# The end of FFN 1 in a hybrid encoder layer: T4 by adding transfers, and the next weights' splits placed around the norms

## The chip, the cores and the metric

The kernel runs on one core of one Trainium2 chip. The metric is the device time of one execution in microseconds; lower is better. It is 1113.76 us before the change (median of 3 runs, 1113.51 to 1113.84).

## The reference

One layer of a streaming encoder on 512 tokens of width 1024, all in float32:

```python
f = swiglu(rms_norm(h, ffn1_pre_g), ffn1_w1, ffn1_w3, ffn1_w2)     # (silu(x@w1) * (x@w3)) @ w2, d_ff 2816
h = h + 0.5 * rms_norm(f, ffn1_post_g)
u = rms_norm(h, mix_pre_g)
q, k, v, xr, xg = split(u @ w_in)
...                                                                # RG-LRU branch, windowed attention, gates, w_o
h = h + 0.5 * rms_norm(swiglu(rms_norm(h, ffn2_pre_g), ...), ffn2_post_g)
```

The change lies in the seam `f @ w2`, the two norms behind it, and the first products of `u @ w_in` (its columns xr).

## The kernel before, in words

**Precision.** Every float32 operand is split into a high and a low part of the matrix format: ScalarE (ACT) copies the high part, VectorE (DVE) subtracts it for the low part. A product is then three matmuls, high x high, high x low, low x high. A 128 x 1024 piece of weights so costs one ACT pass and one DVE pass before TensorE (PE) can use it. `split_dma` makes the low part without VectorE: ACT writes the high part and the negated raw piece, and a DMA from GpSimd's queue (POOL) adds the raw piece from HBM onto it. The set `BY_DMA` names the pieces that are split so.

**Storage.** All big tiles come from one pool of 42 slots of 4 KB a partition. A slot that is asked for while it is still in use makes the asking engine or queue wait for its last user.

**The down projection w2 of FFN 1** is done by seven products of a Strassen-Winograd scheme on halves of the tokens and of the output columns, in the order m1, m5, m2, m6, m3, m7, m4. Each product is cut into G = 5 units of 12 matmuls. `step(u)` prepares units up to u + 4 (`prep(u + LEAD)`, LEAD = 5), runs what `hooks[u]` holds, and then issues the matmuls of unit u; so m1 is steps 0 to 4, m5 5 to 9, m2 10 to 14, m6 15 to 19, m3 20 to 24, m7 25 to 29, m4 30 to 34. Preparing a unit is: split the weights' side (L659 ACT `whi`, L667 DVE `wlo`), split the tokens' side (L213 ACT, L214 DVE), and form the sums and differences that later products need (`sums`). Of the weights' differences, T1 and T2 are made by adding transfers here (`T_load`: L596 ACT negates, L597 POOL's DMA adds), T3 (`b11`) and T4 (`b21`, formed as the units of m6 are prepared) by a DVE pass each (L589). T2 overwrites b22, so m3 loads b22 anew (L673). Two tiles of w2 (2 and 3, `tail`) are multiplied in the plain way (`classical`, L242 to L244).

**The norms.** A tile of 128 tokens is complete when m1 to m6 and the tail (tiles 0 and 1) or m4 and the tail (tiles 2 and 3) are in. `norm(t)` is then one chain over VectorE and ScalarE: add the parts (L294), square and sum (L296), reciprocal root (L259 to L264), new h (L308), square and sum again (L320), root, scaled u (L331 DVE, L332 ACT). PE transposes u (L341), ACT and DVE copy it out as high and low (L351, L353), ACT copies it once more for later (L361). With queues in order, whatever stands in ACT's or DVE's queue ahead of a norm's instruction delays the norm. The order is written out by hand:

- steps 0 to 24; tail on tiles 0 and 1; unit 29 prepared; norm(0);
- steps 25 to 29 (m7); its sum is taken out by DVE (L700), after which m4 may use the banks;
- tail, one column half, on tiles 2 and 3; unit 34 prepared; norm(1);
- m4 on tile 2, transposes of tile 0, tail, norm(2); m4 on tile 3, transposes of tile 1, tail;
- `start`: products with xr0 on the first 256 tokens, transposes of tile 2, norm(3), xr1, one eighth of xr2, transposes of tile 3, the rest of xr2, then the columns 256 to 512 of xr0 and xr1 and so on (L224 to L226).

**The loads and splits of xr0 to xr3** are spread over this by hand. Before the change: xr0 and xr1 are loaded behind step 24 and split by adding DMA in steps 28 and 29 (L159, L160 on ACT, L161 on POOL); xr2 and xr3 are loaded in steps 28 and 29 and split by ACT and DVE (L178, L179) in m4's pass on tile 2, which stands behind norm(1) and ahead of norm(2). `MARKS_A` gives the steps in which the tail is loaded (17, 18), split (21, 22) and the four old h tiles are loaded again (20, 22, 27, 29; L729). SP's queue carries these loads and the spills of the new h (L328, one in each norm), in this order of issue.

Of the kernel before, what the change touches and what calls it, by code (L numbers as in the profile page):

```python
# [51 lines left out]
def hybrid_layer(ctx: ExitStack, tc: tile.TileContext, a: dict, out: bass.AP):  # L52
# [84 lines left out]
    st = {"dma": 0, "split": 0, "get": 0}  # L137
# [226 lines left out]
    def tok_gemm(nm, xs, n, R, gpost_name, scale, gpre_name, first, x_to=None, xf=None, spill=False, then=None, eps=None, pre=None):  # L364

        F = n - R
        acc = {}  # L370
        w = {}

        def accs(t):
            if t not in acc:
                acc[t] = [bank("acc"), bank("acc")]
            return acc[t]

        x_to = x_to or (lambda k: None)
        if not pre:
            both = min(2, F)  # L380
            for k in range(both):
                x_to(k + 1)
                w[k] = get(nm, k, ahead=both - k + 1)
            for tt in ((0, 1), (2, 3)):
                for k in range(both):
                    for t in tt:
                        mm_tok(accs(t), xs[k], t, w[k], k == 0, False)
                        if t % 2:
                            point()
            for k in range(both, F):  # L390
                x_to(k + 2)
                w[k] = get(nm, k, ahead=2 + (R - 2) * (k + 1) // F)
                for t in range(NT):
                    mm_tok(accs(t), xs[k], t, w[k], k == 0, False)
                    if t % 2:
                        point()
        point(True)
        tail = list(pre.hid.seq) if pre else list(range(F, n))
        g, us, trs = [], {}, {}
        ep = lambda t: D * EPS if eps is None else eps[:, t : t + 1]  # L400

        def vectors():
            g.extend((bcast(gpost_name), bcast(gpre_name)))
            if not pre:
                pool.tensor_scalar(out=g[1], in0=g[1], scalar1=NEWT, scalar2=None, op0=ALU.mult)

        def tails():
            for i, k in enumerate(tail):
                x_to(F + i + 1)
                w[k] = get(nm, k, ahead=max(0, len(tail) - 1 - i), rawahead=2)  # L410

        def classical(t, n_):
            for k in tail:
                new = k == tail[0] and (t > 1 and n_ == 1 if pre else k == 0)
                mm_tok(accs(t), xs[k], t, w[k], new, k == tail[-1], (n_,), bool(pre))

        def norm(t, mid=None):
            us[t] = norms(acc[t], t, g[0], scale, g[1], spill, ep(t), mid, pre and pre.part(t), (1, 0) if pre and t > 1 else (0, 1))

        if pre:  # L420
            G = pre.G
            pre.hooks[3 * G].append(vectors)
            for i in range(2):
                pre.hooks[6 * G - 2 + i].append(lambda i=i: [split_to(st["get"] + i + 1), dma_to(st["get"] + i + 3)])
            for u in range(5 * G):
                pre.step(u)
            tails()
            for t in range(2):
                acc[t] = [pre.bank["bc"][t], pre.bank["bx"][t]]
                for n_ in range(2):  # L430
                    classical(t, n_)
            pre.prep(5 * G + LEAD)
            act.activation(g[1], g[1], AF.Copy, scale=NEWT)
            norm(0)
            for u in range(5 * G, 6 * G):
                pre.step(u)
            for t in range(2, 4):
                acc[t] = [pre.bank["bu"][t - 2], bank("acc")]
                classical(t, 1)
            pre.prep(7 * G)  # L440
            pre.hid.eo.clear()
            norm(1)
            for t in range(2, 4):
                for u in range(6 * G, 7 * G):
                    pre.step(u, (t - 2,))
                    if t == 2 and u % G % 2:
                        split_to(st["split"] + 1)
                trs[t - 2] = transpose_mm(us[t - 2])
                transpose_out(trs[t - 2], t - 2, xf if t == 2 else None)
                classical(t, 0)  # L450
                if t == 2:
                    norm(2)
            split_to(st["get"] + len(first))
            dma_to(st["split"] + 2)
            pre.bank.clear()
        else:
            tails()
            vectors()
            split_to(st["get"] + len(first))
            dma_to(st["split"] + 2)  # L460
            for t in range(NT):
                for n_ in range(2):
                    classical(t, n_)
                if t == NT - 1:
                    break
                if t >= 1:
                    trs[t - 1] = transpose_mm(us[t - 1])
                if t == NT - 2:
                    transpose_out(trs[t - 1], t - 1)
                norm(t)  # L470
                if t == 1:
                    transpose_out(trs[t - 1], t - 1, xf)

        t = NT - 1
        ws, bs = [], []

        def start(ks=range(KT)):
            i = len(bs)
            ws.append(get(*first[i], ahead=len(first) - 1 - i, rawahead=2))
            bs.append(bank("f"))  # L480
            if i < len(first) - 1:
                mm_feat(bs[i], ws[i], 0, 256, ks=ks)

        def between():
            transpose_out(trs[t - 1], t - 1, parts=(0,))
            transpose_xf(trs[t - 2], t - 2, xf, (0,))

        start(range(3))
        trs[t - 1] = transpose_mm(us[t - 1])
        mm_feat(bs[0], ws[0], 0, 256, ks=range(3, KT))  # L490
        norm(t, between)
        transpose_out(trs[t - 1], t - 1, parts=(1,))
        transpose_xf(trs[t - 2], t - 2, xf, (1,))
        start()
        start(range(1))
        trs[t] = transpose_mm(us[t])
        transpose_out(trs[t], t)
        transpose_xf(trs[t - 1], t - 1, xf)
        transpose_xf(trs[t], t, xf)
        if then:  # L500
            then()
        k0, k1 = range(KT // 2), range(KT // 2, KT)
        mm_feat(bs[2], ws[2], 0, 256, ks=k0[1:])
        start()
        get_ahead()
        mm_feat(bs[0], ws[0], 256, 512)
        mm_feat(bs[1], ws[1], 256, 512)
        mm_feat(bs[2], ws[2], 256, 512, ks=k0)
        mm_feat(bs[2], ws[2], ks=k1)
        mm_feat(bs[3], ws[3])  # L510
        return bs
# [40 lines left out]
    class Halves:  # L552
# [7 lines left out]
        def __init__(self, nm, hid, hooks, gs, by_add, in_slots, add_t):  # L560
            self.nm, self.hid, self.hooks, self.gs = nm, hid, hooks, gs
            self.by_add, self.in_slots = by_add, in_slots
            self.G = G = len(gs)
            self.loads = [(b, i) for i in range(G) for b in (("b11",) if add_t else ("b11", "b12"))]
            self.first = len(self.loads)
            self.loads += [(b, i) for b in (("b21",) if add_t else ("b22", "b21")) for i in range(G)]
            self.add_t = add_t
            self.again_at = self.names.index("m3") * G - 3
            self.raw, self.ops, self.loaded, self.ready = {}, {}, 0, 0
            self.bank, self.c, self.again, self.did = {}, {}, {}, set()  # L570
# [48 lines left out]
        def sums(self, m, i):  # L619
# [4 lines left out]
            elif m == "m5":  # L624
                if i < T2_EARLY or self.add_t:
                    self.t2(i)
                self.S((0, 0), (0, 1), (0, 0), i)
            elif m == "m2":
                if i >= T2_EARLY and not self.add_t:
                    self.t2(i)  # L630
                self.T("b11", "b22", "b11", i)
                self.S((1, 0), (1, 0), (0, 0), i)
            elif m == "m6":
                self.S((0, 1), (1, 1), (0, 0), i)
                self.T("b21", "b21", "b22", i)
                del self.raw["b22", i]
            elif m == "m7":
                del self.raw["b11", i]
            elif m == "m4":
                del self.raw["b21", i]  # L640

        def prep(self, n, load=True):

            G = self.G
            while self.ready < min(n, 7 * G):
                u = self.ready
                self.ready += 1
                m, i = self.names[u // G], u % G
# [1167 lines left out]
GRAW_AT = (29, 30)  # L1816
TB_AT = (34, 35, 36, 37)

BY_DMA = {("wg", i) for i in range(2)} | {("xr", i) for i in range(2)}

BY_POOL = {("wg", i) for i in range(2, 8)} | {("wk", 0), ("wk", 1)}

# [3 lines left out]
U_SLOTS = 4  # L1826
LOAD_A, LOAD_B = (0, 3, 5, 5), (0, 6, 8, 10)
GS_A = (4, 6), (8, 10), (12, 14), (16, 18), (0, 20)
MARKS_A = (17, 18), (21, 22), (20, 22, 27, 29)
ADD_A = set()  # L1830

TAIL_B = (20, 21)
# [67 lines left out]
```

## Time and profile before

| | |
|---|---|
| median of 3 runs | 1113.76 us |
| profiled execution | 1113.81 us |
| its span | 1112.0 us |
| PE busy | 1094.1 us, 98% |
| DVE busy | 940.6 us, 85% |
| ACT busy | 692.1 us, 62% |
| POOL busy | 398.6 us, 36% |

A share of busy time is an average over the whole span. The change concerns about 262 to 364 us of it. In the rows of the trace that follow, times count from the start of the span; an instruction's row gives start, duration, engine, line, operation and tiles, with the idle time before it and what ended that in brackets. A row of waits gives the sum, how often, and the longest.

### The profile page before, as it was taken

Reading aid. Unit: us, or ns where it says so; the run is one execution under the profiler, and the core shown is the slowest. Engines: PE = TensorE matmul, PEld = TensorE weight load, DVE = VectorE, ACT = ScalarE, POOL = GpSimd, SP = SyncE. Lnnn points to the kernel's source line nnn. Section 1 sums busy time; section 2 is a strip of 40 time slices with the busy share of each in tenths; the row PEclk is TensorE's granted clock in tenths of the full one; section 3 lists DMA queues with packets and bytes.
Section 4 is the critical chain, followed back from the end, with each engine's and each line's share of the span. In section 5 each row is a group of like instructions: output and inputs, shape, how many; then the busy total and the mean of one; then the engine's idle time right before and its main releaser. Section 6 shows DMA issues by size and latency. Waiting matters only on the chain.

```text
span 1112.0 us, 17985 instructions
## 1 busy us (share of the span) xinstructions
PE 1094.1 (98%) x6826; PEld 986.9 (89%) x6826; DVE 940.6 (85%) x1335; ACT 692.1 (62%) x1201; POOL 398.6 (36%) x331
## 2 busy tenths in 40 slices
PE   9999999999988999999999999999999999999997
PEld 8899999988777877899888888888999999998886
DVE  5988999989988978888677866767789989999995
ACT  7756555596666687856656665356555555567672
POOL 0144923230001523133565664010878556521000
PEclk9999999999999999999999999999999999999999
DMA  9324653387553662136322345351423323647642
GB/s 337 119 85 137 144 132 114 132 180 167 178 135 126 173 161 96 57 120 245 98 89 77 95 171 209 104 199 74 146 85 115 96 95 100 204 140 191 181 119 90
DMA packets 51830, 153.30 MB, mean 138 GB/s; under 512 B 5392, under 2 KB 7312, under 8 KB 51744
## 3 DMA queue, kind: packets, MB, share of 16 engines
q1 hardware_dynamic: 43280, 129.57, 34.3%
q0 software_dynamic: 8176, 22.07, 10.5%
q8 instruction: 53, 0.87, 0.3%
q10 hardware_dynamic: 288, 0.52, 0.2%
q14 instruction: 33, 0.27, 0.1%
HBM read 134.32 MB, written 13.62 MB: 133 GB/s over the span
## 4 chain that ended last, share of the span: by engine, by line
PE 94%; DVE 2%; ACT 2%; issue 1%; DMA 0%; DVEq 0%; SPq 0%; ACTq 0%
PE c L806 13%; PE c L807 13%; PE c L808 13%; PE f L224 10%; PE f L226 9%; PE f L225 9%; PE hw L690 5%; PE hw L688 5%; PE hw L689 5%; PE acc L243 1%; PE acc L242 1%; PE acc L244 1%; PE pt L1660 1%; DVE wlo L667 1%; PE s L1624 1%
## 5 line engine op out<-in xcount | busy, mean ns | idle before, releaser
L807 PE MATMUL c<-uT,wlo 128*128 128x256 f32 x516 | 146.0, 283 | 0.0
L808 PE MATMUL c<-uT,whi 128*128 128x256 f32 x516 | 146.0, 283 | 0.0
L806 PE MATMUL c<-uT,whi 128*128 128x256 f32 x516 | 146.0, 283 | 0.0
L806 PE MATMUL c<-Xh,whi 128*128 128x256 f32 x504 | 142.7, 283 | 0.0
L807 PE MATMUL c<-Xh,wlo 128*128 128x256 f32 x504 | 142.6, 283 | 0.0
L224 PE MATMUL f<-uT,whi 128*128 128x512 f32 (+1 forms) x368 | 137.0, 372 | 4.4 <-ACT uT L351 4.4
L226 PE MATMUL f<-uT,whi 128*128 128x512 f32 (+1 forms) x368 | 135.3, 368 | 0.0
L225 PE MATMUL f<-uT,wlo 128*128 128x512 f32 (+1 forms) x368 | 135.2, 367 | 0.0
L808 PE MATMUL c<-Xl,whi 128*128 128x256 f32 x456 | 129.1, 283 | 0.0
L214 DVE TENSOR_TENSOR wlo<-S,whi 128x1024 fp32r<-128x1024 f32 x86 | 121.0, 1407 | 7.3 <-POOL OL L1696 4.5
L213 ACT ACTIVATE whi<-S 128x1024 fp32r<-128x1024 f32 x86 | 88.5, 1055 | 30.2 <-DVE S L855 28.0
L807 PEld LDWEIGHTS c<-uT,wlo 128*128 128x128 f32 x516 | 99.0, 192 | 0.2
L806 PEld LDWEIGHTS c<-uT,whi 128*128 128x128 f32 x516 | 99.0, 192 | 0.2
L808 PEld LDWEIGHTS c<-uT,whi 128*128 128x128 f32 x516 | 99.0, 192 | 0.0
L806 PEld LDWEIGHTS c<-Xh,whi 128*128 128x128 f32 x504 | 96.8, 192 | 0.3 <-issue 0.3
L807 PEld LDWEIGHTS c<-Xh,wlo 128*128 128x128 f32 x504 | 96.8, 192 | 0.0
L689 PE MATMUL hw<-wlo,uT 128*128 128x512 f32 x228 | 88.9, 390 | 0.8 <-DVE wlo L667 0.7
L690 PE MATMUL hw<-whi,uT 128*128 128x512 f32 x228 | 89.1, 391 | 0.2
L688 PE MATMUL hw<-whi,uT 128*128 128x512 f32 x228 | 88.7, 389 | 0.0
L808 PEld LDWEIGHTS c<-Xl,whi 128*128 128x128 f32 x456 | 87.5, 192 | 0.0
L224 PEld LDWEIGHTS f<-uT,whi 128*128 128x128 f32 x368 | 69.8, 190 | 17.3 <-ACT uT L351 4.8
L226 PEld LDWEIGHTS f<-uT,whi 128*128 128x128 f32 x368 | 69.7, 190 | 11.7 <-DVE uT L353 0.2
(435 smaller groups left out, 3177.3 us busy)
## 6 DMA issues: line engine op xcount, KB each, us to landing
raw_w2b<-in_w2b_dram SPq DMA_DIRECT2D x27, 512.0 KB, 4.8
raw_w1b<-in_w1b_dram SPq DMA_DIRECT2D x22, 512.0 KB, 4.2
raw_w3b<-in_w3b_dram SPq DMA_DIRECT2D x22, 512.0 KB, 4.3
raw_w3a<-in_w3a_dram SPq DMA_DIRECT2D x21, 512.0 KB, 4.5
raw_w1a<-in_w1a_dram SPq DMA_DIRECT2D x20, 512.0 KB, 4.4
raw_w2a<-in_w2a_dram SPq DMA_DIRECT2D x17, 512.0 KB, 4.6
raw_wg<-in_wg_dram SPq DMA_DIRECT2D x16, 512.0 KB, 4.0
raw_w2a<-in_w2a_dram POOLq DMA_DIRECT2D x10, 512.0 KB, 9.6
```

The source lines that it names most:

```text
L213: act.activation(hi, src, AF.Copy)
L214: dve.tensor_tensor(out=lo, in0=src, in1=f32(hi), op=ALU.subtract)
L224: pe.matmul(ps[:, c0:c1], wh[:, s], h_, start=k == 0 and c0 == 0, stop=False, skip_group_check=True)
L225: pe.matmul(ps[:, c0:c1], wl[:, s], h_, start=False, stop=False, skip_group_check=True)
L226: pe.matmul(ps[:, c0:c1], wh[:, s], l_, start=False, stop=k == KT - 1, skip_group_check=True)
L242: pe.matmul(acc[n], x[:, 0, c], wh[:, s], start=first, stop=False, skip_group_check=skip)
L688: pe.matmul(ps, xs[:, 0, j, c], hi[:, j, :], start=start and j == 0, stop=False, skip_group_check=True)
L689: pe.matmul(ps, xs[:, 0, j, c], lo[:, j, :], start=False, stop=False, skip_group_check=True)
L690: pe.matmul(ps, xs[:, 1, j, c], hi[:, j, :], start=False, stop=i == self.G - 1, skip_group_check=True)
L806: pe.matmul(ps, wh[:, s], xh, start=first, stop=False, skip_group_check=True)
L807: pe.matmul(ps, wl[:, s], xh, start=False, stop=False, skip_group_check=True)
L808: pe.matmul(ps, wh[:, s], xl, start=False, stop=k == 3, skip_group_check=True)
```

## The change

- **T4 by adding transfers.** In FFN 1 `sums` of m6 no longer subtracts on DVE; `T_load("b21", "b22", i)` takes a new slot, ACT writes -b22 into it, and a DMA of POOL's queue adds b21 from HBM. The first load of b21 is dropped as soon as m2 has used it.
- **`cap`.** `prep` prepares no more than `cap` units; it is 7G - 1 during steps 25 to 29 and 7G otherwise.
- **xr0 and xr1** are loaded in steps 20 and 21 and split by ACT and DVE in steps 22 and 23. **xr2** is loaded in step 27 and split by adding DMA ahead of norm(1). **xr3** is loaded there and split in the second `start`, behind norm(3). The splits in m4's pass on tile 2 and the ones behind the loop go.
- **The h tiles** are loaded in steps 23, 25, 28 and 29.

```diff
-                w[k] = get(nm, k, ahead=max(0, len(tail) - 1 - i), rawahead=2)
+                w[k] = get(nm, k, ahead=max(0, len(tail) - 1 - i), rawahead=0 if pre else 2)
...
-            for i in range(2):
-                pre.hooks[6 * G - 2 + i].append(lambda i=i: [split_to(st["get"] + i + 1), dma_to(st["get"] + i + 3)])
+            x0 = st["get"] + len(tail)
+            for i, u in enumerate(X_AT):
+                pre.hooks[u].append(lambda i=i: dma_to(x0 + i + 1))
+                if i < 2:
+                    pre.hooks[u + 2].append(lambda i=i: split_to(x0 + i + 1))
...
             norm(0)
+            pre.cap = 7 * G - 1
             for u in range(5 * G, 6 * G):
                 pre.step(u)
+            pre.cap = 7 * G
...
             pre.prep(7 * G)
             pre.hid.eo.clear()
+            split_to(x0 + 3)
+            dma_to(x0 + 4)
             norm(1)
             for t in range(2, 4):
                 for u in range(6 * G, 7 * G):
                     pre.step(u, (t - 2,))
-                    if t == 2 and u % G % 2:
-                        split_to(st["split"] + 1)
...
-            split_to(st["get"] + len(first))
-            dma_to(st["split"] + 2)
...
-            ws.append(get(*first[i], ahead=len(first) - 1 - i, rawahead=2))
+            ws.append(get(*first[i], ahead=min(len(first) - 1 - i, 2 if pre else 3), rawahead=2))
...
                 self.T("b11", "b22", "b11", i)
                 self.S((1, 0), (1, 0), (0, 0), i)
+                if self.add_t:
+                    del self.raw["b21", i]
             elif m == "m6":
                 self.S((0, 1), (1, 1), (0, 0), i)
-                self.T("b21", "b21", "b22", i)
+                if self.add_t:
+                    self.T_load("b21", "b22", i)
+                else:
+                    self.T("b21", "b21", "b22", i)
...
-            while self.ready < min(n, 7 * G):
+            while self.ready < min(n, self.cap):
...
-BY_DMA = {("wg", i) for i in range(2)} | {("xr", i) for i in range(2)}
+BY_DMA = {("wg", i) for i in range(2)} | {("xr", 2)}
...
-MARKS_A = (17, 18), (21, 22), (20, 22, 27, 29)
+MARKS_A = (17, 18), (21, 22), (23, 25, 28, 29)
+X_AT = (20, 21, 27)
```

More of the change, by code (lines that the diff above doesn't have):

```diff
@@ L566, in __init__ @@
             self.loads += [(b, i) for b in (("b21",) if add_t else ("b22", "b21")) for i in range(G)]
-            self.add_t = add_t
+            self.add_t, self.cap = add_t, 7 * G
             self.again_at = self.names.index("m3") * G - 3
```

## The prediction

> **What bounds the kernel now.** I read the page first, then who made TensorE wait, then the stretches around the end of FFN 1, then VectorE and ScalarE in order of time.
>
> ```profile
> span 1112.0 us, 17985 instructions
> PE 94%; DVE 2%; ACT 2%; issue 1%; DMA 0%; DVEq 0%; SPq 0%; ACTq 0%
> ```
>
> TensorE carries 94% of the chain, so the kernel is worth what its matmuls cost, and the change touches no matmul. All that it can win is time in which TensorE stands still. The waits of TensorE over the whole span:
>
> ```profile
> PE f L224 <- ACT uT L351: 4.4, 1, 4.4
> PE hw L688 <- DVE hc L700: 2.9, 1, 2.9
> PE hw L243 <- DVE wlo L179: 1.3, 1, 1.3
> PE hw L689 <- DVE wlo L667: 0.7, 1, 0.7
> ```
>
> These four, 9.3 us together, are also the whole answer for 240 to 370 us alone: the down projection of FFN 1 and its norms, the code that is changed. After the 4.4 us wait the clock falls too:
>
> ```profile
> 242.00:252.00 10.00, 10.00 (x46) 8.29 (x45) 9.14 (x12) 10.00 (x14) 4.21 (x4) 1.00 1.10 269
> 262.00:272.00 10.00, 10.00 (x46) 8.29 (x45) 10.00 (x14) 6.02 (x8) 0.00 (x0) 1.00 0.31 71
> 272.00:282.00 10.00, 10.00 (x46) 8.19 (x45) 10.00 (x12) 4.75 (x6) 1.12 (x2) 1.00 0.75 247
> 352.00:362.00 10.00, 10.00 (x72) 9.78 (x73) 8.84 (x20) 7.06 (x18) 0.00 (x0) 0.85 0.56 192
> ```
>
> (Columns: stretch, length, busy PE, PEld, DVE, ACT, POOL, granted clock, DMA share, GB/s.) A clock of 0.85 over the last ten microseconds is another 1.5 us of TensorE's time. So 9.3 + 1.5 = 10.8 us is the most that can come back. The same rows say who causes it: DVE is busy 10.00 of 10.00 us from 262 to 282, ACT only 6.02 and 4.75. VectorE is late when the norms begin, and from there the four norms run one behind another on VectorE and ScalarE; TensorE waits for that chain at the places above. A gain is therefore counted along that chain, up to the transposes of the fourth norm, not at TensorE.
>
> **First term: work that VectorE loses and gets before the first norm.** The difference T4 of m4 is one of the L589 passes; five of the ten lie in the units of m6.
>
> ```profile
> L596 ACT ACTIVATE raw_w2a<-raw_w2a x10: 1042/1050/1056, 222.8 to 250.1; 128x1024 f32<-128x1024 f32 x10
> L597 POOL DMA_DIRECT2D raw_w2a<-in_w2a_dram x10: 1195/1204/1291, 224.5 to 251.4; - x10
> L589 DVE TENSOR_TENSOR raw_w2a<-raw_w2a,raw_w2a x10: 1217/1219/1222, 253.8 to 285.7; 128x1024 f32<-128x1024 f32 x10
> ...
> L673 SPq DMA_DIRECT2D raw_w2a<-in_w2a_dram x5: 367/367/368, 267.8 to 281.6; - x5
> ...
> DMA to landing us min/median/max: 3.6/7.4/12.8
> ```
>
> ```profile
> 271.82 1.22 DVE L589 TENSOR_TENSOR raw_w2a<-raw_w2a,raw_w2a 128x1024 f32<-128x1024 f32 x1
> 272.96 1.22 DVE L667 TENSOR_TENSOR wlo<-raw_w2a,whi 128x1024 fp32r<-128x1024 f32 x1
> ...
> 291.54 1.22 DVE L667 TENSOR_TENSOR wlo<-raw_w2a,whi 128x1024 fp32r<-128x1024 f32 x1
> ...
> 295.62 1.22 DVE L667 TENSOR_TENSOR wlo<-raw_w2a,whi 128x1024 fp32r<-128x1024 f32 x1
> ...
> 310.12 0.69 DVE L294 TENSOR_TENSOR hc<-hw,hc 128x512 f32<-128x512 f32 x1
> ...
> 320.22 1.23 DVE L667 TENSOR_TENSOR wlo<-raw_w2a,whi 128x1024 fp32r<-128x1024 f32 x1 [0.95 <-ACT whi L659]
> ...
> 321.96 1.22 DVE L667 TENSOR_TENSOR wlo<-raw_w2a,whi 128x1024 fp32r<-128x1024 f32 x1
> ...
> 326.53 1.23 DVE L667 TENSOR_TENSOR wlo<-raw_w2a,whi 128x1024 fp32r<-128x1024 f32 x1 [1.00 <-ACT whi L659]
> ...
> 328.27 1.28 DVE L700 TENSOR_TENSOR hc<-hw,hc 128x512 f32<-128x512 f32 x2
> 329.89 1.23 DVE L667 TENSOR_TENSOR wlo<-raw_w2a,whi 128x1024 fp32r<-128x1024 f32 x1 [0.34 <-ACT whi L659]
> ...
> 331.63 0.68 DVE L294 TENSOR_TENSOR hc<-hw,hc 128x512 f32<-128x512 f32 x1
> ```
>
> From one start to the next a pass takes 272.96 - 271.82 = 1.14 us. Five leave: 5.70 us. The first two xr weights are now split by ACT and DVE in steps 22 and 23, ahead of the first norm (L294 at 310.12): 2 x 1.14 = 2.28 us come in. If VectorE stays as packed as it is, the first norm starts 3.42 us earlier, at 306.70. The waits of 0.7 and 1.3 us that VectorE's lateness caused go with it, so TensorE has the first norm's sums ready in time.
>
> What the five passes turn into costs, beside other work: five L596 passes on ACT, 5 x 1.05 = 5.2 us, where ACT has 20 - 6.02 - 4.75 = 9.2 us free; five issues on POOL, 5 x 1.20 = 6.0 us, where POOL shows 0.00 and 1.12 of 10, ahead of the two gain loads of step 15 and nothing else; and five transfers. The two extra ACT passes for xr0 and xr1 lie before an ACT idle of 4.27 us (first row below). With that cover gone they would delay the first norm one to one. The raw b21 slots are free from m2 to m6, then taken again by the negated copies: as many in use at the end as now.
>
> **Second term: ScalarE between the first and second norm.**
>
> ```profile
> 310.90 0.64 ACT L296 ACTIVATE junk<-hc 128x512 f32<-128x512 f32 x1 [4.27 <-DVE hc L294]
> ...
> 332.41 0.63 ACT L296 ACTIVATE junk<-hc 128x512 f32<-128x512 f32 x1 [2.04 <-DVE hc L294]
> ...
> 338.77 0.72 ACT L332 ACTIVATE hg<-hg,r 128x512 f32<-128x512 f32 x1 [0.60 <-DVE r L264]
> 339.40 1.99 ACT L178 ACTIVATE whi<-raw_xr 128x1024 fp32r<-128x1024 f32 x2
> ...
> 350.64 0.72 ACT L332 ACTIVATE hg<-hg,r 128x512 f32<-128x512 f32 x1 [0.66 <-DVE r L264]
> ...
> 360.33 0.58 ACT L361 ACTIVATE xf<-tr 128x512 f32<-128x512 f32 x1
> 361.23 1.09 ACT L351 ACTIVATE uT<-tr 128x512 fp32r<-128x512 f32 x2 [0.31 <-PE tr L341]
> ```
>
> Steps 28 and 29 put four ACT passes for xr0 and xr1 (L159 and L160) ahead of the splits of m4's last two units; that is VectorE's idle of 1.00 and 0.34 us. Five units at 321.96 - 320.22 = 1.74 us and the two L700 (1.28 us) would need 9.98 us from 320.22 to L294, and it takes 331.63 - 320.22 = 11.41. With the passes gone the second norm starts 1.4 us earlier still. Two passes for xr2 come in ahead of it (L178's two take 1.99 us), under ACT's idle of 2.04 us and in the place of the four that leave; if xr2's load were late, the norm would wait for it one to one. In SP's queue that load now stands behind the first h spill and the load of h[1], which itself moves from step 22 to 25, behind that spill. The spill goes out before the first norm ends at 320.22, and the second begins 11.41 us later (9.98 after the change): time for two loads that land in 3.6 to 7.4 us.
>
> The new `cap` does nothing: with a lead of five, step 29 prepares 34 units with or without it, and L700 at 328.27 stands ahead of the last L667 at 329.89 already. Zero, with nothing to uncover.
>
> **Third term: between the second and third norm.** Here xr2 and xr3 are split today (L178 at 339.40, 1.99 us, and two VectorE passes behind).
>
> ```profile
> 343.95 0.68 DVE L294 TENSOR_TENSOR hc<-acc,hc 128x512 f32<-128x512 f32 x1
> ...
> 353.08 0.68 DVE L294 TENSOR_TENSOR hc<-acc,hc 128x512 f32<-128x512 f32 x1
> ...
> 361.86 1.29 DVE L353 TENSOR_TENSOR uT<-tr,uT 128x512 fp32r<-128x512 f32 x2 [0.20 <-ACT uT L351]
> ```
>
> After the third norm, with nothing between, the next L294 follows its L332 by 353.08 - 350.64 = 2.44 us. After the second it takes 343.95 - 338.77 = 5.18. The difference, 2.74 us, goes.
>
> **Fourth term: xr3's split is now behind the fourth norm but ahead of the copies of its transposes.** ACT would run L361 (360.33 to 360.9), the split (0.95), then L351 at 361.9 instead of 361.23; VectorE waits for the split, spends 1.14 on it, and L353 starts near 363.05 instead of 361.86. TensorE:
>
> ```profile
> 360.59 1.03 PE L341 MATMUL tr<-ident,hg 128*128 128x128 f32 x8
> ...
> 361.58 0.28 PE L225 MATMUL f<-uT,wlo 128*128 128x256 f32 x1
> 361.70 0.28 PE L226 MATMUL f<-uT,whi 128*128 128x256 f32 x1
> ```
>
> Nine matmuls at 0.12 us after the transposes, then two of the next group, and at 362.7 it needs the first L353, which ends at 363.65: 0.9 us lost. Bounds: nothing, if the tail of the copies hides it, to 0.95 + 1.14 = 2.1 us if both passes lie bare.
>
> **The sum.** 3.42 + 1.4 + 2.74 - 0.9 = 6.7 us off the profiled execution's 1113.81 (span 1112.0 and 1.81 around it; the median of the runs is 1113.76): **1107.1 us**. The chain sets this, not TensorE: without all its waits TensorE would be at the transposes of 360.59 by 360.59 - 10.8 = 349.8, the chain gets there at 360.59 - 7.56 = 353.0, so some 3 us of waits stay, split among m4's start, xr0 and the fourth norm's transposes. Behind them TensorE shows no wait, so the shift lasts to the end.
>
> The stall of 2.90 us left the clock at 1.00 and that of 4.42 us did not. [...]
>
> **Rivals.**
>
> *The lead is capped by slots.* VectorE needs ACT's high halves first, and ACT waits for slots:
>
> ```profile
> 284.16 1.06 ACT L659 ACTIVATE whi<-raw_w2a 128x1024 fp32r<-128x1024 f32 x1 [2.50 <-PE hw L689]
> ```
>
> This is m3's third unit: done at 285.2, and VectorE would come for it at 291.54 - 5.70 = 285.8 (the L667 of 291.54 above). 0.6 us is all there is. If the new order of slots ties such a pass to one unit later (12 matmuls, of which the stretches above hold 46 in 10 us: 2.6 us), 2.0 us of the first term go and the time is 1109.1; two units, 4.6 us, 1111.7. For it: the wait is there. Against: other such passes wait for L589, which is gone, and slots fall free earlier.
>
> *Transfers collide, and it gets slower.* m3 reloads b22 by the five L673 loads from 267.8 to 281.6, just when five adding transfers are added. At 242 to 252, under the ten adding transfers, the DMA share was 1.10 and landing took up to 12.8 us. The last reload, issued at 281.6, is needed for the split that VectorE now does at 295.62, then 289.9, less 1.05 for ACT: 288.85, so 7.2 us of landing are free. At 12.8 us the loss is 5.6 and the time 1112.7; from 13.9 us on the change loses; at 17 us it is 1116.9. Against: shares of 0.31 and 0.75 leave 9.4 us of the engines' time between 262 and 282, where the row of 242 leaves none, and five transfers are half of ten. [...]
>
> **How the numbers follow.** What a measurement can tell from no change is about 0.2%, 2.2 us. Forecast (1105.2 to 1108.5): 0.62. Capped lead: 0.24, of which 0.19 is still faster by over 0.2%. Collision: 0.14, 0.04 within 0.2% and 0.10 slower. Faster 0.81, same 0.09, slower 0.10. The range runs from 1105.2 (the fourth term at its lower bound gives 1106.2, and a wait or two elsewhere, 1.00 us for such a one above, may go with the new order of slots) to 1111.5, short of two units of capped lead; the fourth term's upper bound, 1108.3, lies inside.
>
> **What would show it.** VectorE's first L294 near 306.7, the second near 326.8, the third near 336.4; between the second norm's L332 and the third L294 2.4 us; waits of TensorE at m4's start about 2 us, at xr0 under 2 us, at the first matmuls on columns 256 to 512 a new one near 0.9 us for L353; clock 1.00 from 342 to 362; reloads L673 landing within 7 us. I am wrong if the first L294 stays above 309 (capped lead, or late reloads: the idle before ACT's L659 tells which), or if a wait appears behind 370 us that was not there.

## The result and the profile after

The changed kernel takes 1108.61 us (median of 5 runs, 1108.24 to 1109.83) where the kernel before takes 1113.82 (1113.51 to 1114.71): ratio 0.9955 (95% interval 0.994 to 0.9969). Measured once more beside other kernels the ratio was 0.9942 (0.9929 to 0.9954). The forecast was 1107.1. The change is faster, by 5.0 to 6.5 us or about half a per cent, and both intervals lie wholly below 1; the forecast said 6.7.

The page of the changed kernel, its span and its chain by engine (before: 1112.0 us and 94% TensorE):

```profile
span 1106.8 us, 18012 instructions
PE 96%; DVE 2%; ACT 1%; issue 0%; DMA 0%; DVEq 0%; SPq 0%; ACTq 0%
```

Who made TensorE wait between 240 and 370 us (line, cause, us in all, times, longest). This is the whole answer:

```profile
PE hw L696 <- DVE hc L708: 3.5, 1, 3.5
PE f L226 <- DVE uT L353: 0.9, 1, 0.9
PE tr L341 <- DVE hg L331: 0.5, 1, 0.5
```

Lines 560 and up have moved by three to eight (L688 is L696, L700 is L708, L667 is L675, L659 is L667). Of the four waits of before, 9.3 us, three are gone: the two small ones ahead of the first norm and the 4.4 us at xr0. The one at m4's start has grown from 2.9 to 3.5, and the 0.9 us for the second L353 is new, as forecast.

The stretches, with the columns that the prediction names (granted clock third from the right, then DMA share and GB/s):

```profile
262.00:272.00 10.00, 10.00 (x45) 8.26 (x44) 10.00 (x13) 10.00 (x13) 4.08 (x4) 1.00 0.67 131
...
282.00:292.00 10.00, 10.00 (x46) 8.29 (x45) 9.33 (x12) 7.21 (x12) 0.00 (x0) 1.00 1.06 354
...
322.00:332.00 10.00, 6.53 (x17) 5.12 (x17) 9.56 (x17) 5.71 (x11) 0.87 (x1) 0.66 0.58 136
```

VectorE is no longer packed: 9.33 of 10 from 282 on. ScalarE, 6.02 of 10 busy from 262 to 272 before, is now at 10.00. The half clock, at xr0 before, now stands in m4 (0.66).

VectorE in order of time (start, us, line, tiles; in brackets the idle ahead and its cause):

```profile
249.33 1.23 DVE L675 TENSOR_TENSOR wlo<-raw_w2a,whi 128x1024 fp32r<-128x1024 f32 x1 [0.86 <-ACT whi L667]
...
290.33 1.23 DVE L675 TENSOR_TENSOR wlo<-raw_w2a,whi 128x1024 fp32r<-128x1024 f32 x1 [0.67 <-ACT whi L667]
...
298.98 1.23 DVE L179 TENSOR_TENSOR wlo<-raw_w2a,whi 128x1024 fp32r<-128x1024 f32 x1 [0.26 <-ACT whi L178]
...
307.61 0.69 DVE L294 TENSOR_TENSOR hc<-hw,hc 128x512 f32<-128x512 f32 x1
...
327.61 0.68 DVE L294 TENSOR_TENSOR hc<-hw,hc 128x512 f32<-128x512 f32 x1
...
336.56 1.29 DVE L353 TENSOR_TENSOR uT<-tr,uT 128x512 fp32r<-128x512 f32 x2 [1.08 <-ACT uT L351]
337.77 0.68 DVE L294 TENSOR_TENSOR hc<-acc,hc 128x512 f32<-128x512 f32 x1
...
346.83 0.68 DVE L294 TENSOR_TENSOR hc<-acc,hc 128x512 f32<-128x512 f32 x1
```

The first row serves as a mark: it is the same pass in both kernels, and up to it the order of instructions is the same on every engine. Before, it stood at 249.68:

```profile
249.68 1.23 DVE L667 TENSOR_TENSOR wlo<-raw_w2a,whi 128x1024 fp32r<-128x1024 f32 x1 [0.86 <-ACT whi L659]
```

So 0.35 us of the earlier first L294 is no work of the change. Counted from the mark, the first norm begins after 58.28 us, 60.44 before: 2.16 us earlier, not 3.42. The next distances are 20.00 (21.51 before), 10.16 (12.32) and 9.06 (9.13).

The two idle times of VectorE (0.67 and 0.26 us) followed up on ScalarE, in order of time:

```profile
289.24 1.06 ACT L667 ACTIVATE whi<-raw_w2a 128x1024 fp32r<-128x1024 f32 x1 [0.56 <-DMA raw_w2a<-in_w2a_dram]
294.93 1.06 ACT L667 ACTIVATE whi<-raw_w2a 128x1024 fp32r<-128x1024 f32 x1 [1.17 <-PE hw L698]
297.37 0.63 ACT L213 ACTIVATE hT<-kept 128x512 fp32r<-128x512 f32 x1 [0.85 <-PE hw L697]
...
308.39 0.63 ACT L296 ACTIVATE junk<-hc 128x512 f32<-128x512 f32 x1 [1.88 <-DVE hc L294]
```

The first of these passes waits for the last reload of b22, the next two for slots that TensorE still reads; the last row is for later. Both rivals of the prediction, collision and capped lead, are there, each small.

### The profile page after: what moved, and what is told of

The parts are those of the page before. It is cut to its first block, busy times and chain, and to the rows that moved or that the text cites. A ratio compares the mean times of both kernels' runs of the same rounds, so it can differ in the third digit from the quotient of the medians.

```text
span 1106.8 us, 18012 instructions
## 1 busy us (share of the span) xinstructions
PE 1093.1 (99%) x6826; PEld 987.1 (89%) x6826; DVE 936.2 (85%) x1331; ACT 695.6 (63%) x1205; POOL 403.9 (36%) x335
## 4 chain that ended last, share of the span: by engine, by line
PE 96%; DVE 2%; ACT 1%; issue 0%; DMA 0%; DVEq 0%; SPq 0%; ACTq 0%
PE c L814 13%; PE c L815 13%; PE c L816 13%; PE f L224 9%; PE f L226 9%; PE f L225 9%; PE hw L696 6%; PE hw L697 6%; PE hw L698 6%; PE acc L243 1%; PE acc L242 1%; PE acc L244 1%; PE pt L1668 1%; PE s L1632 1%; PE s L1631 1%; PE o L1684 1%
## 5 line engine op out<-in xcount | busy, mean ns | idle before, releaser
L696 PE MATMUL hw<-whi,uT 128*128 128x512 f32 x228 | 88.7, 389 | 0.0
```

The source lines that it names most:

```text
L696: pe.matmul(ps, xs[:, 0, j, c], hi[:, j, :], start=start and j == 0, stop=False, skip_group_check=True)
```

## The experiments

The theory: the four norms hang on one chain of VectorE and ScalarE, so what an edit is worth is read as a change of one of the distances along it (mark to first L294, then from L294 to L294). The table has what all kernels showed; the ratio is to the kernel before on the same chip. "Half clock" is how long the trace's record of the granted clock stood at 0.5 between 240 and 370 us.

| kernel | to 1st | to 2nd | to 3rd | to 4th | half clock, us | ratio (95%) |
|---|---|---|---|---|---|---|
| before | 60.44 | 21.51 | 12.32 | 9.13 | 3.41 | 1 |
| changed | 58.28 | 20.00 | 10.16 | 9.06 | 6.83 | 0.9955 (0.994 to 0.9969) |
| changed_again | 58.29 | 20.00 | 9.55 | 9.06 | 3.41 | 0.9942 (0.9929 to 0.9954) |
| sched_only | 62.71 | 19.99 | 9.92 | 9.06 | 6.83 | 0.9988 (0.9979 to 0.9997) |
| t4_only | 55.66 | 21.51 | 12.32 | 9.13 | 3.41 | 0.9956 (0.9943 to 0.9968) |
| xr3_behind | 58.26 | 19.99 | 9.56 | 9.06 | 3.41 | 0.9937 (0.9925 to 0.995) |
| m7_sum_first | 58.27 | 20.00 | 9.56 | 9.05 | 6.83 | 0.995 (0.9937 to 0.9964) |
| reload_early | 57.39 | 19.99 | 9.56 | 9.06 | 3.41 | 0.9935 (0.9922 to 0.9949) |
| xr_by_transfers | 59.35 | 19.99 | 9.55 | 9.06 | 3.41 | 0.9952 (0.9939 to 0.9964) |
| three_together | 59.34 | 20.00 | 9.56 | 9.06 | 3.41 | 0.9948 (0.9935 to 0.996) |
| splits_between | 58.28 | 20.00 | 12.29 | 9.05 | 2 x 3.41 | 0.9959 (0.9946 to 0.9971) |
| xr3_and_reload | 57.37 | 19.99 | 9.56 | 9.05 | 0 | 0.9928 (0.9914 to 0.9941) |
| xr3_reload_m7 | 57.37 | 19.99 | 9.56 | 9.05 | 3.41 | 0.9931 (0.9919 to 0.9943) |
| one_more_transfer | 59.65 | 19.98 | 9.57 | 9.06 | 3.41 | 0.9959 (0.9945 to 0.9972) |

**The two halves of the change.** The schedule without T4, then T4 without the schedule (`sched_only` is the changed kernel less the lines below, `t4_only` the kernel before with the same lines added).

```diff
 # sched_only
-                if self.add_t:
-                    del self.raw["b21", i]
...
-                if self.add_t:
-                    self.T_load("b21", "b22", i)
-                else:
-                    self.T("b21", "b21", "b22", i)
+                self.T("b21", "b21", "b22", i)
```

> The changed kernel with m4's T4 back on VectorE (five L592 passes in m6's units, raw b21 kept from m2 to m6); the new places of the splits stay. Chain theory (VectorE and ScalarE set the time, the places add up): against the changed kernel VectorE gets 5 x 1.14 = 5.70 us back and loses the idle of about 1.25 us that T4 by transfers brought, so the first L294 comes some 4.5 us later (near 312.1 on the changed trace's clock of 307.61), the distances behind it stay, and the time is 1108.6 + 4.5 = 1113.1, within 0.7 of the kernel before. Rival (the new places of the splits earn most, because the two added VectorE passes lie in idle time): 1110.5 or less, the first L294 not later than 310.1.

> The kernel before with m4's T4 by adding transfers and nothing else. Chain theory: VectorE loses 5.70 us ahead of the first norm, of which about 1 us comes back as idle behind reloads and slots, so the first L294 moves from 310.12 to about 305.4, the distances of the three norms behind it stay 21.5, 12.3 and 9.1, and the time is 1113.8 - 4.7 = 1109.1. Rival one (transfers and slots eat the term): the first L294 stays above 308 and the time is 1111.5 or more. Rival two (TensorE's own work becomes the bound, so an earlier chain earns less than its shift): first L294 near 305.4, but the time 1110.5 or more.

VectorE in order of time, of `sched_only` and of `t4_only`:

```profile
312.17 0.68 DVE L294 TENSOR_TENSOR hc<-hw,hc 128x512 f32<-128x512 f32 x1
...
332.16 0.68 DVE L294 TENSOR_TENSOR hc<-hw,hc 128x512 f32<-128x512 f32 x1
```

```profile
249.31 1.23 DVE L672 TENSOR_TENSOR wlo<-raw_w2a,whi 128x1024 fp32r<-128x1024 f32 x1 [0.86 <-ACT whi L664]
...
290.46 1.23 DVE L672 TENSOR_TENSOR wlo<-raw_w2a,whi 128x1024 fp32r<-128x1024 f32 x1 [0.82 <-ACT whi L664]
...
304.97 0.68 DVE L294 TENSOR_TENSOR hc<-hw,hc 128x512 f32<-128x512 f32 x1
...
326.48 0.69 DVE L294 TENSOR_TENSOR hc<-hw,hc 128x512 f32<-128x512 f32 x1
```

Both theories' numbers were met within 0.5 us: 312.17 for 312.1, 304.97 for 305.4, 1112.96 us and 1109.39 us. The schedule costs 62.71 - 60.44 = 2.27 us ahead of the first norm (two passes of 1.14 were forecast) and gives back 1.5 and 2.4 behind it. T4 alone takes 60.44 - 55.66 = 4.78 us away, not 5.70, and leaves every distance behind it as it was. Its one idle of 0.82 us (ScalarE waits there for the last reload) explains 0.90 of the 0.92 us that are missing: a pass lasts 1.22 us and the next starts after 1.14, so an idle costs its own length and this overlap of 0.08. So T4 is nearly all of the gain: 0.9956 alone, 0.9955 and 0.9942 with the schedule, where the schedule alone is 0.9988. The halves do not quite add up ahead of the first norm: -4.78 + 2.27 = -2.51, the changed kernel has -2.16. The slot wait of 0.26 us at 298.98 is in neither of the two.

**The collision.** If the 0.67 us of idle come from late reloads, an earlier reload must take them away.

```diff
-            self.again_at = self.names.index("m3") * G - 3
+            self.again_at = self.names.index("m3") * G - (4 if add_t else 3)
```

> The changed kernel with m3's reloads of b22 issued one unit earlier. Collision theory (the five adding transfers make the last reload land late): VectorE's idle of 0.67 us at 290.3 falls below 0.2, the first L294 comes 0.5 to 0.7 us earlier (near 307.0) and the time is 0.5 lower than the changed kernel's. Rival (slots: each reload now holds a slot one unit longer): the idle behind ScalarE's slot waits grows from 0.26 to 0.8 or more, the first L294 stays at 307.6 or comes later, the time is the same or higher.

VectorE of `reload_early`, in order of time; the second row is its only idle between 250 us and the first L294 that the timeline marks:

```profile
249.51 1.23 DVE L675 TENSOR_TENSOR wlo<-raw_w2a,whi 128x1024 fp32r<-128x1024 f32 x1 [0.86 <-ACT whi L667]
...
295.93 1.23 DVE L675 TENSOR_TENSOR wlo<-raw_w2a,whi 128x1024 fp32r<-128x1024 f32 x1 [0.27 <-ACT whi L667]
...
306.90 0.68 DVE L294 TENSOR_TENSOR hc<-hw,hc 128x512 f32<-128x512 f32 x1
```

The idle of 0.67 is gone, and the first norm comes 58.29 - 57.39 = 0.90 us earlier than in `changed_again`: somewhat more than expected. With the overlap the idle was worth 0.75, and a third gap of 0.08 us, which the timeline of the changed kernel does not mark, went with it. The slot wait of 0.26 at 298.98 came back as 0.27 in another place. With 60.44 - 57.39 = 3.05 the term now lies 0.37 from its forecast of 3.42.

Why the reloads were late shows in the DMA issues of 255 to 300 us (transfers, count, KB, median us to landing): before, changed, and, for the reloads' queue alone, `sched_only` and `t4_only`:

```profile
raw_w2a<-in_w2a_dram SPq DMA_DIRECT2D x7, 512.0 KB, 4.3
...
bc_mix_pre_g<-in_mix_pre_g_dram POOLq DMA_DIRECT2D x1, 512.0 KB, 4.9
```

```profile
raw_w2a<-in_w2a_dram SPq DMA_DIRECT2D x7, 512.0 KB, 8.3
raw_w2a<-in_w2a_dram POOLq DMA_DIRECT2D x5, 512.0 KB, 9.9
...
bc_mix_pre_g<-in_mix_pre_g_dram POOLq DMA_DIRECT2D x1, 512.0 KB, 15.7
```

```profile
raw_w2a<-in_w2a_dram SPq DMA_DIRECT2D x7, 512.0 KB, 3.8
```

```profile
raw_w2a<-in_w2a_dram SPq DMA_DIRECT2D x7, 512.0 KB, 8.4
```

The late landing comes with T4's transfers (8.4 us with them alone) and not with the new places of the loads and splits (3.8).

POOL issues the five adding transfers between 264.29 and 274.14, one every 2.4 to 2.6 us; they land at 271.77, 275.70, 279.04, 282.79 and 286.82, one every 3.3 to 4.0 us. A queue that is fed faster than it is served grows: 7.5 us to landing for the first, 12.7 for the last, 15.7 for the gain load behind them. And m3's five reloads, between 3.6 and 4.9 us before and between 3.7 and 4.2 in `sched_only`, take 4.3 us for the first and 8.1 to 9.4 for the other four.

**One transfer more.** `one_more_transfer` is `xr3_and_reload` (below) with `ADD_A = {("m6", 4)}`: another low half by an adding transfer, where ScalarE had idle time.

> The one with xr3 behind and the reloads earlier, and the low half of m6's last unit also made by ScalarE and an adding transfer instead of VectorE. Chain theory: ScalarE stands idle 1.66, 1.14, 1.14 and 1.34 us at 275 to 287 behind TensorE's slots, so one pass of 1.05 fits, VectorE loses 1.14, and the first L294 comes up to 1.1 us earlier, 56.3 us behind the L675 with the idle of 0.86 us; time about 1.0 below the one with two edits, 0.9919 of the kernel before. Rival (ScalarE is as late as VectorE by now, as it was with xr0 and xr1 by transfers; it waits for slots, not for work): VectorE waits for ScalarE's high halves instead, the first L294 comes at most 0.4 us earlier, and the time is the same or higher.

It got slower, and for a reason that neither theory names. Who made TensorE wait in 240 to 370 us (the first two of three lines), then ScalarE and VectorE in order of time:

```profile
PE hw L696 <- DVE hc L708: 3.2, 1, 3.2
PE hw L697 <- DMA wlo<-raw_w2a: 1.3, 1, 1.3
```

```profile
286.22 1.06 ACT L667 ACTIVATE whi<-raw_w2a 128x1024 fp32r<-128x1024 f32 x1 [5.42 <-issue]
```

```profile
287.31 1.23 DVE L675 TENSOR_TENSOR wlo<-raw_w2a,whi 128x1024 fp32r<-128x1024 f32 x1 [2.16 <-ACT whi L667]
```

The added transfer, issued at 274.96 behind four others, lands after 11.2 us at 286.15. TensorE waits 1.3 us for it. ScalarE stands idle for 5.42 us up to 286.22; the profile names no cause ("issue"), but it goes on right behind that landing, so that it waited for it is likely and not shown. VectorE waits for ScalarE, and the first norm begins 2.28 us later (59.65 for 57.37). This is the mechanism of the prediction's second rival: at this place one adding transfer more costs more than the VectorE pass of 1.14 us that it saves.

**xr0 and xr1 by transfers again**, at the changed places, and this together with two other edits:

```diff
-BY_DMA = {("wg", i) for i in range(2)} | {("xr", 2)}
+BY_DMA = {("wg", i) for i in range(2)} | {("xr", i) for i in range(3)}
```

> The changed kernel with the low halves of xr0 and xr1 made by ScalarE and an adding transfer (as in the kernel before), at the changed places. Chain theory: VectorE loses 2 x 1.14 = 2.28 us ahead of the first norm, ScalarE gets two passes more (2.1 us) under its idle there, first L294 near 305.3, the distances behind it as in the changed kernel, wait at m4's start near 1.2 us instead of 3.5 with the clock at 1.00, time 2.3 to 2.9 us below the changed kernel's. Rival one (the two transfers and ScalarE's passes come at a bad place, so the first norm waits for ScalarE instead): first L294 at 306.8 or later, time within 1 us of the changed kernel's. Rival two (TensorE becomes the bound): first L294 near 305.3 but the time lowered by less than 1.2.

> The changed kernel with xr3's split behind the transposes' copies, one more unit of m4 behind m7's sum, and xr0 and xr1 by adding transfers. Chain theory: what each earns alone adds up, as all lie on the same chain at different places: about 1.3, 0.6 and 2.3 us, so 4.2 us below the changed kernel's time, 1104.8. Rival (TensorE has less than that left to lose: its waits of 4.9 us and the half clock are all there is, and some of them cannot go): 2.5 us below, and no wait of VectorE longer than 0.5 ahead of the transposes is left for TensorE.

VectorE of `xr_by_transfers`:

```profile
301.57 1.23 DVE L675 TENSOR_TENSOR wlo<-raw_w2a,whi 128x1024 fp32r<-128x1024 f32 x1 [1.62 <-ACT whi L667]
...
304.94 1.23 DVE L675 TENSOR_TENSOR wlo<-raw_w2a,whi 128x1024 fp32r<-128x1024 f32 x1 [1.54 <-ACT whi L667]
...
308.42 0.68 DVE L294 TENSOR_TENSOR hc<-hw,hc 128x512 f32<-128x512 f32 x1
```

My theory failed here. VectorE loses two passes of 1.14 and waits 1.62 + 1.54 = 3.16 us for ScalarE instead: ScalarE is as late as VectorE once T4 is off VectorE, and its two more passes of 1.05 come onto the chain. The first norm begins 1.06 us later (59.35 for 58.29), and the time is 1109.31 us for the changed kernel's 1108.29 in the same round: close to rival one. `three_together` has the same 59.34, and at 1108.64 us it misses its 4.2 us below the changed kernel and its rival's 2.5 too. What the change does, two ScalarE passes turned into two VectorE passes at that place, is right for it.

**The norms behind.** First xr2 and xr3 back between the second and third norm, both by VectorE; then xr3's split behind the copies of the last transposes.

```diff
 # splits_between                                    # and BY_DMA without xr
-            split_to(x0 + 3)                        # ahead of norm(1)
...
+                    if t == 2 and u % G % 2:        # in m4's first pass
+                        split_to(st["split"] + 1)
```

> The changed kernel with the splits of xr2 and xr3 back between the second and third norm, both by VectorE (in the steps of m4's first pass, as in the kernel before); xr0, xr1 and T4 as changed. Chain theory: the first L294 stays near 307.5 and the second 20.0 behind it, the third comes 12.3 us after the second instead of 9.6, and TensorE's wait of 0.9 us for L353 goes: 2.74 - 0.9 = 1.8 us above the changed kernel, 0.9958 of the kernel before. Rival (the transposes of TensorE at the lower clock end last there anyway, so the splits fit beside them): the third L294 at most 10.7 behind the second, the time within 0.5 us of the changed kernel's or below it.

The rows of `splits_between` on VectorE that carry the verdict:

```profile
327.54 0.68 DVE L294 TENSOR_TENSOR hc<-hw,hc 128x512 f32<-128x512 f32 x1
...
336.35 2.36 DVE L179 TENSOR_TENSOR wlo<-raw_xr,whi 128x1024 fp32r<-128x1024 f32 x2 [0.95 <-ACT whi L178]
...
339.83 0.68 DVE L294 TENSOR_TENSOR hc<-acc,hc 128x512 f32<-128x512 f32 x1
```

12.29 us instead of 9.55, and a ratio of 0.9959 where 0.9958 was expected: the third term is 2.74 us as forecast.

```diff
 # xr3_behind, in start()
-            ws.append(get(*first[i], ahead=min(len(first) - 1 - i, 2 if pre else 3), rawahead=2))
+            ws.append(get(*first[i], ahead=(2, 1, 0, 0)[i] if pre else len(first) - 1 - i, rawahead=3 if pre and i in (1, 2) else 2))
```

> The changed kernel with xr3's split put behind the copies of the fourth norm's transposes instead of ahead of them. Chain theory: the wait of TensorE for L353 (0.9 us) goes and the time is 1107.7; no new wait, since xr3 is used only by the last group of matmuls there. Rival (the copies are late by themselves, because they wait for the transposes): the wait stays at 0.5 us or more and the time within 0.4 of 1108.6. A third way: the split comes late for its own use or for what ScalarE does next, and a wait for L179 appears behind 360 us: 1108.6 or more.

All that TensorE waits for in 240 to 370 us in `xr3_behind`:

```profile
PE hw L696 <- DVE hc L708: 3.5, 1, 3.5
PE tr L341 <- DVE hg L331: 0.9, 1, 0.9
```

The wait of 0.9 for L353 is gone and none takes its place. So the fourth term was real and could be had back. The time alone would not show it: 0.9937 lies within the interval of the changed kernel's second measurement. The span does: from the fourth L294 to its end it takes 760.0 us in both traces of the changed kernel and in the three other kernels with that wait 760.0 to 760.1, but 758.9 in `xr3_behind` and in the kernel before. The term is worth 1.1 us.

**m4's start and the clock.** One unit more behind m7's sum (`pre.cap = 7 * G - 2`), alone and on top of the two edits that helped.

> The changed kernel with one more of m4's units prepared behind m7's sum (the cap one lower), so that the two L708 stand one unit, 1.74 us, earlier on VectorE and nothing is added or taken away. Theory with the clock in it: TensorE's wait at m4's start falls from 3.5 to about 1.8 us, the granted clock stays at 1.00 from 322 to 332 (0.66 in the changed kernel), the transposes of the first tile are in time, VectorE's idle of 1.08 us ahead of L353 shrinks to about 0.5, and the time is 1108.0. Rival (the chain on VectorE alone counts, the slow clock lies inside waits that it leaves anyway): wait and clock change as said, the time stays within 0.2 of 1108.6. Rival two (the unit that moves behind is now late for m4's matmuls): a wait for its L675 appears, and the time is 1109 or more.

All of TensorE's waits in `m7_sum_first`, 240 to 370 us, and two stretches:

```profile
PE f L224 <- ACT uT L351: 2.9, 1, 2.9
PE hw L696 <- DVE hc L708: 1.7, 1, 1.7
```

```profile
322.00:332.00 10.00, 8.30 (x41) 6.99 (x42) 9.55 (x17) 5.65 (x11) 0.87 (x1) 1.00 0.54 123
342.00:352.00 10.00, 7.11 (x36) 6.81 (x36) 8.44 (x21) 7.53 (x21) 0.94 (x2) 0.66 0.47 151
```

The wait at m4's start halves as expected and the clock stays up there. The 1.8 us turn up at xr0, where TensorE now waits 2.9 us, and the half clock follows it there. The third norm comes 9.56 behind the second, but `changed_again` has 9.55 without the edit, so the edit earned nothing on the chain. From the fourth L294 to the end it takes 760.1 us as in the changed kernel, although the wait of 0.9 for L353 is gone; the half clock now lies there (344.1 to 350.9 us), which fits. The time, 0.995 (0.9937 to 0.9964), does not differ from the changed kernel's two measurements.

**The changed kernel again, and the best version.**

> The changed kernel once more, unaltered, beside the others. Time: 0.9955 of the kernel before. [...]

The copies of the first tile's transposes: VectorE's row in `changed_again` (its idle was 1.08 us in the first trace), then ScalarE's row in the first trace, where TensorE is late:

```profile
335.75 1.29 DVE L353 TENSOR_TENSOR uT<-tr,uT 128x512 fp32r<-128x512 f32 x2 [0.49 <-ACT uT L351]
```

```profile
335.93 1.09 ACT L351 ACTIVATE uT<-tr 128x512 fp32r<-128x512 f32 x2 [0.48 <-PE tr L341]
```

Same wait of 3.5 us, half clock of 3.41 us this time, VectorE's idle 0.49 us for 1.08, and the third norm 9.55 behind the second: the 0.6 us by which the first trace missed the third term belong to that execution, not to the kernel.

`xr3_and_reload` has both edits that helped, `xr3_reload_m7` the lower cap on top.

> The changed kernel with xr3's split behind the copies of the fourth norm's transposes and m3's reloads one unit earlier. Chain theory: the two are at different places of the chain and add up, 1.0 and 0.8 us below the changed kernel's time, so 0.9926 of the kernel before, near 1106.5; first L294 near 306.9 and no wait of TensorE for L353. Rival (TensorE is the bound by now): 0.9935 or more.

> The one with xr3 behind and the reloads earlier, and one more of m4's units behind m7's sum. [...] The chain on VectorE is as long as without the edit, so the time is within 0.3 us of the one with two edits. Rival (a shorter wait at m4's start is worth its length in the end): 0.7 us or more below the one with two edits.

TensorE's waits in `xr3_and_reload`, 240 to 370 us, complete:

```profile
PE hw L696 <- DVE hc L708: 2.6, 1, 2.6
PE f L224 <- ACT uT L351: 1.2, 1, 1.2
PE tr L341 <- DVE hg L331: 0.9, 1, 0.9
PE f L226 <- DVE uT L353: 0.2, 1, 0.2
```

The wait of 0.9 us for L353 is gone as expected; the 0.2 us are another one, at xr0. 1106.32 us (1105.98 to 1106.88), ratio 0.9928 (0.9914 to 0.9941), expected 0.9926: it beats the kernel before clearly, and all five of its runs lie below all five of either measurement of the changed kernel (1107.67 at the lowest), though on another occasion. In `xr3_reload_m7` the waits are 2.9 at xr0 and 0.8 at m4's start, 3.7 in all for 4.9, and one half clock of 3.41 us comes in for it: 1106.65 us, the same. The chain is as long as without the edit.

## Why the prediction was right, and where not

**The bound was right.** In every kernel of the table the chain of VectorE and ScalarE through the norms moved as its distances say and the time with it: from the fourth L294 to the end of the span it takes 758.9 to 760.1 us in all fourteen traces. In the changed kernel no new wait of TensorE appeared behind 370 us. The prediction's list of waits is that of 240 to 370 us; over the whole span the kernel before has two more, of 1.1 and 0.2 us, in its first 22 us, where nothing changes.

**First term: mis-sized, 2.16 for 3.42.** The passes were counted right: xr0 and xr1 cost 2.27 us for 2.28 (`sched_only`). The step that failed is "if VectorE stays as packed as it is". T4 by transfers brought 4.78 of 5.70, the two halves together lost another 0.35, and 0.90 of the missing 1.26 came back when the reloads went out one unit earlier. The rest, 0.37, is the slot wait of 0.27 us that stayed and the overlap of 0.08 that every idle costs besides.

**The reloads' landing: the forecast "within 7 us" was wrong.** The rival gave 7.2 us of landing as free; the last reload took 9.4. That is 2.2 us too late, but it was issued earlier, 30.45 us behind the mark (at 279.78) for 31.92 (at 281.6), so 0.7 us were left, and VectorE's idle is 0.67. I took the landing times of before (3.6 to 4.9 us for the five reloads) as if they were properties of the transfers; beside T4's adding transfers they were 4.3 to 9.4. The case did not decide the sign, but it came, as did the slot wait, each for a part of a microsecond where I had priced them as whole cases.

**ScalarE's cover was thinner than written.** The idle of 4.27 us ahead of L296 in the trace before is 1.88 in the changed kernel. I had named it as what hides ScalarE's added passes; it did for the changed kernel, and `xr_by_transfers` shows that it does for no more.

**Second term: right.** 1.51 us for 1.4, in `sched_only` and the changed kernel alike.

**Third term: right in the kernel, short in one profile.** 2.77 us for 2.74 in `changed_again`, 2.16 in the first trace. There ScalarE and VectorE waited 0.6 us longer for TensorE's transposes of the first tile, behind an m4 that ran at half clock for 6.83 us. I had expected a wait of about 2 us at m4's start, with the clock at 1.00 behind it as behind the 2.90 us of before. It was 3.5: TensorE reaches m4 4.2 us earlier than before (321.65 for 325.81), having lost its waits of 0.7 and 1.3 and shorter ones beside them, and L708 starts only 3.6 us earlier (324.68 for 328.27).

**Fourth term: right in place, 1.1 us for 0.9.** **The cap: right, nothing, by the code.** Step 29 asks for 34 units and a cap of 34 takes none away; no run leaves it out alone.

**The sum.** By the chain, 2.16 + 1.51 + 2.16 + 0.07 - 1.1 = 4.8 us in the first trace and 2.15 + 1.51 + 2.77 + 0.07 - 1.1 = 5.4 in the second, for 6.7 forecast. The mark itself came 0.35 and 0.57 us earlier than before, which is chance, as nothing of the change acts by then. With it the spans are met: 5.2 us in the first trace (1112.0 to 1106.8) and 6.0 in the second (1112.0 to 1106.0). The forecast time of 1107.1 was 1.5 us below the first measurement: 1.26 are the reloads with the slot wait, 0.6 the clock, 0.2 the fourth term, and about half a microsecond came back, most of it by the mark's chance.

## What to carry to other kernels

When work is moved from an engine to a queue of transfers, price the queue by its rates: how often it is fed, how often it serves, and what else then lands later (here m3's reloads, 8.1 to 9.4 us for 3.6 to 4.9); landing times from a stretch in which the queues were little used do not tell it. After the busiest engine has lost work, look again at the next one, since its idle time before is not its idle time after. A wait that is shortened at one place of a chain moves to the next place, unless the chain itself becomes shorter.

## What was not expected of the hardware

**A half clock lasted 3.41 or 6.83 us, and the length of the wait ahead of it did not tell alone whether it came.** Every half clock in these fourteen traces between 240 and 370 us lasted 3.41 or 6.83 us. Each of the eight waits of TensorE of 3.2 to 4.5 us there was followed by one, none of the waits of 1.7 us and less was. In between it went both ways: the clock fell after 1.9 us (`t4_only`, m4's start), 2.3 (`splits_between`), 2.6 (`reload_early`), 2.8 (`three_together`), 2.9 (`m7_sum_first`) and 2.9 (`xr3_reload_m7`), and it did not after 2.6 (`xr3_and_reload`), 2.8 (`t4_only`, xr0) and 2.9 (before, m4's start). The wait of 2.6 us at m4's start was followed by a half clock of 3.41 us in `reload_early` and by none in `xr3_and_reload`, with the same order of instructions up to there. What decides between the two is not shown.

In the changed kernel the matmuls of m4 start 0.43 us apart at half clock and 0.23 at full clock. So a half clock behind a wait cost TensorE up to an estimated 1.7 us more (half of 3.41), and twice that where it lasted 6.83; 0.6 us of it reached the chain in the trace of the changed kernel.

**Plain loads beside adding transfers landed late.** Four of m3's five reloads took 8.1 to 9.4 us from issue to landing beside T4's adding transfers, where they took 3.6 to 4.9 before and 3.7 to 4.2 in `sched_only`. The five adding transfers of 512 KB landed 3.3 to 4.0 us apart there. How much of that spacing is the adding and how much the reloads beside them, no run separates.
